# A diffusion transformer block on one core: state space work of layer 0 gathered on VectorE, with merged tables and scans

## The chip, the cores and the metric

One NeuronCore of a Trainium2 chip runs the whole program. TensorE (PE) multiplies matrices, VectorE (DVE), ScalarE (ACT) and GpSimd (POOL) do the elementwise work, and SyncE (SP) issues the transfers. The metric is the device time of one execution in microseconds (us), lower is better.

## The reference, cut to what matters

Two layers, each over 512 latent tokens and 256 context tokens of width 1024. Each layer conditions its normalised input with a shift and a scale from an adaptive projection (ada), mixes tokens in three ways side by side (windowed attention, a gated convolution of three taps, a bidirectional state space model), and then runs an MLP.

```python
mod = (c_act @ w_ada[l] + b_ada[l])[:, None, :]
a_lat = modulate(rms_norm(h, g_pre_mix), sh1, sc1)
...
conv = cb * centred_conv3(cc * cx, conv_w)
# s5_bidirectional
lam_bar = jnp.exp(lam * dt)
b_bar = ((lam_bar - 1) / lam)[..., None] * lax.complex(b_re, b_im)
h_lat_f = diag_scan(lam_bar[0], drive(u, 0), h_ctx_f[:, -1], False)
h_lat_b = diag_scan(lam_bar[1], drive(u, 1), h_ctx_b[:, 0], True)
y = real(einsum(hf, c_mat[0]) + einsum(hb, c_mat[1])) + d_skip * t
g = jax.nn.gelu(y)
return g * jax.nn.sigmoid(g @ w_glu + b_glu)
```

The state space model has 16 groups, 64 complex states each, two directions. Layer 1 gives no context output.

## The kernel before, in words

Every large product is made of three matmuls (`mm3`, L659 to L661) on a high and a low part of both operands, so each weight tile is split into such parts first (`wload`: cast on ACT, L643, and the subtraction of the low part, L644, in turn on DVE and POOL).

The tokens are cut into chunks of 8, 96 chunks in all (`NCH`; 32 of them context). The state space model is done in two halves of 8 groups. For a half, `ssm_mats` builds matrices from powers of the eigenvalues (DVE and POOL, L353 to L359; PE, L367 to L387). The last products of PE give the kernel of a chunk, which goes to DRAM (`strips`) and comes back as a Toeplitz matrix (`ssm_tr`, `ssm_tm`). `ssm_scan` multiplies the input chunks by these matrices (PE, L483), turns the result by a table of phases (`ssm_table`), runs a real scan over the chunks (L503), and turns back (L513 to L520) to the state `s`. `ssm_read` adds the chunk's own part (L539) and the state's (L545) and applies the gelu.

A tile framework puts the instructions of each engine into an order of its own by a modelled timeline, and places its waits by the tiles. So the code's order is only a hint, and the orders below are what the engines get. Each engine works through its own order without overtaking.

The program in stages, by the trace: `startup` (0 to about 81 us: norms, the first two slices of the ada projection in two halves `ada_half`, conditioning of the input by `transpose_mod`, the projection `u_proj` of the state space input, and `ssm_mats`), `phase_w` of layer 0 (to 204.4 us: convolution, both scans and readouts, further ada slices, L774), attention, the MLP of layer 0 with the preparation of layer 1's matrices and tables in its shadow (`ssm_spill`), then the same of layer 1 with `phase_w` from about 1056 to 1131 us. In `transpose_mod` a letter for each block of 128 channels says which engine does what: ACT or DVE makes the conditioned block (`full`, L729 on DVE) and its high part, DVE or POOL subtracts (L734). One half of the ada projection is eight tiles of 512 KB, each used by four matmuls (L817), whose sum is added to a bias (L820), transposed and made into the scale `A` (L829).

Of the kernel before, what the change touches and what calls it, by code (L numbers as in the profile page):

```python
# [95 lines left out]
def ssm_params(E, a):  # L96
# [196 lines left out]
def ssm_table(E, l, d, a0, na, tab):  # L293

    nc = E.nc
    V, G = nc.vector, nc.gpsimd
    c0 = (l * 2 + d) * 8 + a0
    cs = slice(c0, c0 + na)
    tb = tab if d == 0 else tab[:, :, :, ::-1]
    G.memset(tb[:, 0, :, 0:1], 1.0)  # L300
    G.memset(tb[:, 1, :, 0:1], 0.0)
# [2 lines left out]
    while m < NCH:
        n = min(m, NCH - m)
        wrb, wib = bc(wr, 2, n), bc(wi, 2, n)
        t1 = E.mp.tile([P, 8, 32], F32, name="ssm_tt", tag="ssm_y", bufs=2)[:, :na, :n]
        t2 = E.mp.tile([P, 8, 32], F32, name="ssm_tt", tag="ssm_y", bufs=2)[:, :na, :n]
        ar, ai = tb[:, 0, :, 0:n], tb[:, 1, :, 0:n]
        o_r, o_i = tb[:, 0, :, m:m + n], tb[:, 1, :, m:m + n]  # L310
        V.tensor_mul(o_r, ar, wrb)
        G.tensor_mul(t1, ai, wib)
        V.tensor_sub(o_r, o_r, t1)
        G.tensor_mul(o_i, ar, wib)
        G.tensor_mul(t2, ai, wrb)
        V.tensor_add(o_i, o_i, t2)
        m *= 2
        if m < NCH:
            nw = E.mp.tile([P, 4, 8], F32, name="ssm_w", tag="ssm_w", bufs=2)[:, :, :na]
            V.tensor_mul(nw[:, 2], wr, wr)  # L320
            V.tensor_mul(nw[:, 3], wi, wi)
            V.tensor_sub(nw[:, 0], nw[:, 2], nw[:, 3])
            V.scalar_tensor_tensor(out=nw[:, 1], in0=wr, scalar=2.0, in1=wi, op0=OP.mult, op1=OP.mult)
            wr, wi = nw[:, 0], nw[:, 1]
# [648 lines left out]
def block(E, l, cols):  # L973
    tc, nc, a = E.tc, E.nc, E.a
    with psum_phase(E, f"w{l}", s=3, a=1, m=4) as E.pp, \
# [548 lines left out]
```

## Time and profile before

| | us |
|---|---|
| median of three runs (lowest, highest) | 1680.35 (1680.06, 1680.41) |
| the profiled execution | 1681.77 |
| its span in the trace | 1679.9 |
| PE busy in the span | 1569.0 |
| DVE, ACT, POOL busy | 904.7, 538.8, 502.8 |

The span is the stretch from the first to the last instruction of the trace, and 1.87 us of the profiled execution lie outside it. Busy time is the time in which an engine runs at least one instruction. PE's instructions are pipelined, so a busy PE is not PE at its best, and its granted clock is 1.00 or 0.50 of full speed in a stretch.

### The profile page before, as it was taken

The numbers are of one execution on the slowest core, as the hardware profiler recorded it, in microseconds if no ns is written. First come the engines' busy times: TensorE is split into PE (matmuls) and PEld (weight loads), VectorE is DVE, ScalarE is ACT, GpSimd is POOL, SyncE is SP. The second block draws the span as 40 slices with busy tenths as digits, with TensorE's granted clock in tenths as the row PEclk, the third lists the DMA queues.
The fourth block names the chain that finished last, engine by engine and source line by source line (L and its number), as shares of the span: only waits on it lengthen the run. The fifth ranks groups of instructions, "written<-read, shape, count | busy, mean of one in ns | idle before, by whom it ended". The sixth has DMA issues, their size and how long they took to land. (4 is left out here: it accounts for less than half of the span.)

```text
span 1679.9 us, 22886 instructions
## 1 busy us (share of the span) xinstructions
PE 1569.0 (93%) x8872; PEld 1265.2 (75%) x8872; DVE 904.7 (54%) x1949; ACT 538.8 (32%) x1005; POOL 502.8 (30%) x509
## 2 busy tenths in 40 slices
PE   5899898899899999999999997999889899999997
PEld 2587686677878888878688885778667788888885
DVE  8837626775894483323233358473774833333335
ACT  4220225553622131111213236112554522322232
POOL 5745622003372261111112125453102321222222
PEclk9888798999999999999999998979999899999999
DMA  8455422003333141162713135742302232222223
GB/s 307 154 191 184 137 70 76 1 12 128 126 114 110 44 146 60 51 221 80 251 51 100 51 138 194 278 148 85 114 1 95 84 101 98 101 100 101 90 99 125
DMA packets 73132, 193.82 MB, mean 115 GB/s; under 512 B 15168, under 2 KB 25664, under 8 KB 72768
## 3 DMA queue, kind: packets, MB, share of 16 engines
q1 hardware_dynamic: 73024, 192.37, 33.2%
q8 instruction: 69, 1.13, 0.3%
q14 instruction: 39, 0.32, 0.1%
HBM read 172.15 MB, written 20.19 MB: 114 GB/s over the span
## 5 line engine op out<-in xcount | busy, mean ns | idle before, releaser
L644 POOL TENSOR_TENSOR w<-w 128x1024 fp32r<-128x1024 f32 x86 | 208.7, 2426 | 727.8 <-ACT w L643 332.9
L643 ACT CAST w<-w 128x1024 fp32r<-128x1024 f32 x172 | 178.9, 1049 | 469.9 <-PE ps_q L660 296.0
L660 PE MATMUL ps_q<-w,f 128*128 128x512 f32 x640 | 249.9, 392 | 3.9 <-DVE w L644 3.1
L659 PE MATMUL ps_q<-w,f 128*128 128x512 f32 x640 | 247.6, 392 | 2.7 <-DVE g L1476 2.6
L661 PE MATMUL ps_q<-w,f 128*128 128x512 f32 x640 | 247.7, 391 | 0.0
L644 DVE TENSOR_TENSOR w<-w 128x1024 fp32r<-128x1024 f32 x86 | 110.4, 1283 | 147.0 <-ACT w L643 138.0
L659 PE MATMUL ps_m<-g,w 128*128 128x256 f32 (+1 forms) x544 | 177.9, 332 | 2.5 <-DVE g L731 2.4
L660 PE MATMUL ps_m<-g,w 128*128 128x256 f32 (+1 forms) x544 | 179.4, 331 | 0.0
L661 PE MATMUL ps_m<-g,w 128*128 128x256 f32 (+1 forms) x544 | 177.9, 330 | 0.0
L660 PE MATMUL ps_m<-f,w 128*128 128x512 f32 (+1 forms) x464 | 172.0, 371 | 2.0 <-DVE f L734 1.6
L659 PE MATMUL ps_m<-f,w 128*128 128x512 f32 (+1 forms) x464 | 171.1, 372 | 1.5 <-ACT f L725 1.2
L661 PE MATMUL ps_m<-f,w 128*128 128x512 f32 (+1 forms) x464 | 170.2, 368 | 0.0
L1482 DVE TENSOR_TENSOR g<-g,ps_q 128x1024 f32<-128x1024 f32 x60 | 73.3, 1221 | 177.3 <-PE ps_q L661 177.3
L660 PEld LDWEIGHTS ps_q<-w,f 128*128 128x128 f32 x640 | 120.7, 189 | 30.4 <-DVE w L644 4.6
L659 PEld LDWEIGHTS ps_q<-w,f 128*128 128x128 f32 x640 | 120.2, 188 | 29.1 <-DVE g L1476 3.9
L661 PEld LDWEIGHTS ps_q<-w,f 128*128 128x128 f32 x640 | 120.7, 189 | 24.7
L659 PE MATMUL ps_m<-w,f 128*128 128x512 f32 (+1 forms) x336 | 125.2, 375 | 8.8 <-DVE p L929 4.1
L661 PE MATMUL ps_m<-w,f 128*128 128x512 f32 (+1 forms) x336 | 124.7, 372 | 0.0
L660 PE MATMUL ps_m<-w,f 128*128 128x512 f32 (+1 forms) x336 | 123.5, 369 | 0.0
L1405 DVE SCALAR_TENSOR_TENSOR relu<-ps_m,relu 128x512 f32<-128x512 f32 (+1 forms) x104 | 58.3, 564 | 118.8 <-ACT relu L1404 118.7
L1408 DVE TENSOR_TENSOR f<-relu,f 128x512 fp32r<-128x512 f32 (+1 forms) x104 | 85.1, 820 | 57.8 <-ACT f L1407 57.4
L659 PEld LDWEIGHTS ps_m<-g,w 128*128 128x128 f32 x544 | 103.7, 193 | 16.3 <-DVE g L731 3.0
(289 smaller groups left out, 2762.8 us busy)
## 6 DMA issues: line engine op xcount, KB each, us to landing
w<-in_w_ada SPq DMA_DIRECT2D x96, 512.0 KB
w<-in_w_mlp_in SPq DMA_DIRECT2D x64, 512.0 KB
w<-in_w_mlp_out SPq DMA_DIRECT2D x64, 512.0 KB
w<-in_w_out SPq DMA_DIRECT2D x16, 512.0 KB
w<-in_w_conv SPq DMA_DIRECT2D x12, 512.0 KB
h_d<-g SPq DMA_DIRECT2D x12, 512.0 KB
w<-in_w_q SPq DMA_DIRECT2D x8, 512.0 KB
f<-h_d SPq DMA_DIRECT2D x8, 512.0 KB
```

The costliest lines, as they stand in the source:

```text
L643: nc.scalar.copy(hi, raw)
L644: (nc.gpsimd if turn % 2 else nc.vector).tensor_sub(lo, raw, hi.bitcast(F32))
L659: nc.tensor.matmul(out, lh, rh, start=first, stop=False)
L660: nc.tensor.matmul(out, lh, rl, start=False, stop=False)
L661: nc.tensor.matmul(out, ll, rh, start=False, stop=last)
L1405: V.scalar_tensor_tensor(out=s, in0=pt, scalar=0.0, in1=s, op0=OP.max, op1=OP.mult)
L1408: V.tensor_sub(lo, s, hi.bitcast(F32))
L1482: V.tensor_add(facc[t], facc[t], pq)
```

## The change

- `ssm_params`, `ssm_mats`, `ssm_out_mat`, `ssm_scan`: the halves that POOL did go to DVE, two copies go to ACT.
- `ssm_table` builds one table for both directions (the backward one reads it reversed) in fewer and longer steps, all on DVE. In layer 0 it is called in `startup`.
- The scans of one direction, eight of 96 elements, become two of 384 with a zero in the decay at each edge. The turning back becomes two products of 760 elements, one difference and one sum.
- The second half's eight ada tiles of `startup` go to state space tiles that nothing uses yet, not to the pool of weight tiles. A transpose uses another PSUM tile.
- The matrices of the second half of layer 0 are made after the first half's readout, not in `startup`.
- `wload` subtracts on DVE alone up to the end of `phase_w`. `transpose_mod` in `startup` has its subtractions all on DVE, and half of its blocks made on ACT. The gelu has one DVE instruction less, one convolution tap goes to ACT, its last subtraction to DVE, two memsets to POOL. `E.steps` sets which ada steps stand between which parts.

```diff
-    wr, wi = E.w8[:, 0, cs], E.w8[:, 1, cs]
+    V.tensor_copy(tab[:, :, :, 1], E.w8[:, :, cs])
     m = 1
...
+    while m < NCH - 1:
+        k = min(m, 24, NCH - 1 - m)
+        t = E.mp.tile([P, 2, n, 24], F32, name="ssm_tt", tag="T3", bufs=2)[:, :, :, :k]
+        a, o = tab[:, :, :, 1:1 + k], tab[:, :, :, m + 1:m + 1 + k]
+        br, bi = (bc(tab[:, q, :, m], 2, k) for q in range(2))
+        for q in range(2):
+            V.tensor_mul(o[:, q], a[:, q], br)
+            V.tensor_mul(t[:, q], a[:, 1 - q], bi)
+        V.tensor_sub(o[:, 0], o[:, 0], t[:, 0])
+        V.tensor_add(o[:, 1], o[:, 1], t[:, 1])
+        m += k
...
-        G.tensor_add(z[:, 0], z[:, 0], t[:, 0])
-        G.tensor_sub(z[:, 1], z[:, 1], t[:, 1])
...
+        V.tensor_add(z[:, 0], z[:, 0], t[:, 0])
+        V.tensor_sub(z[:, 1], z[:, 1], t[:, 1])
+        rz = E.mp.tile([P, 4, NCH], F32, name="ssm_rz", tag="T3", bufs=2)
+        V.tensor_copy(rz, bc(E.r8[:, u.cs], 2, NCH))
...
-                V.tensor_tensor_scan(o, r8, i, 0.0, OP.mult, OP.add)
+            zq = z[:, q].rearrange("p k c -> p (k c)")[:, rv]
+            V.tensor_tensor_scan(zq, rf, zq, 0.0, OP.mult, OP.add)
...
-            G.tensor_copy(s[:, :, :, 0:CCH], s[:, :, :, NCH:NCH + CCH])
+            nc.scalar.copy(s[:, :, :, 0:CCH], s[:, :, :, NCH:NCH + CCH])
...
-        (nc.gpsimd if turn % 2 else nc.vector).tensor_sub(lo, raw, hi.bitcast(F32))
+        (nc.gpsimd if turn % 2 and E.wpool else nc.vector).tensor_sub(lo, raw, hi.bitcast(F32))
...
-        raw = wtile(E, [P, 2, 512])
+        if h == 0:
+            raw = wtile(E, [P, 2, 512])
+        elif kc in (4, 5, 6):
+            raw = E.xa([P, 2, 512])
...
-    E.smode = "oppooppo"
+    E.smode = "eoeoeoeo"
...
-    E.steps = ((2, 2, 2, 5, 6), (1, 1, 1, 3, 4))
+    E.steps = ((0, 2, 2, 5, 8), (1, 1, 1, 3, 4))
...
-    E.U1 = ssm_mats(E, E.S, 0, 1)
...
-        U1 = E.U1
         ssm_read(E, U0, t0, s0, u_t, 0, y_d, not both)
+        U1 = ssm_mats(E, S, 0, 1)
```

The lines of the changed kernel have other numbers. In the pieces of its orders, a name's number only tells one buffer from another.

DVE, in the conditioning of the second half of the ada projection. Before, L820 adds the bias, L827 copies the transposed sums, and L829 makes `A`, with the table's steps (L311 to L323) between:

```order
207 L820 TENSOR_TENSOR f4_454<-f4_454,ps_a_604 128x256
208 L313 TENSOR_TENSOR ssm_tab0_1026<-ssm_tab0_1026,ssm_tt_1206 128x8x32
209 L316 TENSOR_TENSOR ssm_tab0_1026<-ssm_tab0_1026,ssm_tt_1207 128x8x32
210 L320 TENSOR_TENSOR ssm_w_1237<-ssm_w_1224 128x8
211 L827 COPY mod00_398<-ps_a_654 128x2x2x2 x2
212 L321 TENSOR_TENSOR ssm_w_1237<-ssm_w_1224 128x8
213 L313 TENSOR_TENSOR ssm_tab1_1027<-ssm_tab1_1027,ssm_tt_1216 128x8
214 L323 SCALAR_TENSOR_TENSOR ssm_w_1237<-ssm_w_1224 128x8
215 L829 SCALAR_TENSOR_TENSOR A00_401<-mod00_398,vecs_75 128x2x4
```

Now the addition stands at row 228 (its line is L808), the copies are L815, `A` is L817, and L624 is the subtraction of a weight's low part, here of the convolution's:

```order
231 L624 TENSOR_TENSOR w_1009<-w_1004,w_1008 128x1024
232 L624 TENSOR_TENSOR w_1013<-w_1006,w_1012 128x1024
233 L305 TENSOR_TENSOR ssm_tab_854<-ssm_tab_854,ssm_tt_900 128x16x24
234 L306 TENSOR_TENSOR ssm_tab_854<-ssm_tab_854,ssm_tt_900 128x16x24
235 L815 COPY mod00_398<-ps_s_654 128x2x2x2 x2
236 L278 TENSOR_TENSOR ssm_t_846<-ssm_b_835,ssm_fz_85 128x256
237 L279 TENSOR_TENSOR ssm_t_847<-ssm_b_835,ssm_fz_85 128x256
238 L303 TENSOR_TENSOR ssm_tab_854<-ssm_tab_854 128x16x15 x2
239 L304 TENSOR_TENSOR ssm_tt_907<-ssm_tab_854 128x16x15 x2
240 L817 SCALAR_TENSOR_TENSOR A00_401<-mod00_398,vecs_75 128x2x4
```

Two weight subtractions and longer table steps have come between the addition and `A`, and the small squarings `ssm_w` are gone.

PE, at the end of the matrices of the second half. Before, L377 and L379 are their last products, and the first half's input products (L483, from `ssm_xt_869` and `ssm_xt_891`) and its first own part (L539) follow:

```order
364 L377 MATMUL ps_s_1012<-ssm_cb_941,ssm_x_969 128x32
365 L379 MATMUL ps_s_1012<-ssm_cb_941,ssm_x_969 128x32
366 L483 MATMUL ps_s_1302<-u_t_1025,ssm_xt_869 64x96 x8
367 L483 MATMUL ps_s_1303<-u_t_1025,ssm_xt_869 64x96 x8
368 L774 MATMUL ps_a_1033<-w_1699,cT_74 32x256 x2
...
376 L539 MATMUL ps_s_1409<-u_t_1025,ssm_tm_938 128x96
```

Now those products are L357 and L359, the input products L463, the ada steps L755 and the own part L520, and all of these are of the second half:

```order
512 L359 MATMUL ps_s_1299<-ssm_cb_1228,ssm_x_1256 128x32
513 L463 MATMUL ps_s_1419<-u_t_1002,ssm_xt_1243 64x96 x8
514 L463 MATMUL ps_s_1420<-u_t_1002,ssm_xt_1243 64x96 x8
515 L755 MATMUL ps_a_1607<-w_1802,cT_74 32x256 x4
516 L755 MATMUL ps_a_1607<-w_1803,cT_74 32x256
517 L463 MATMUL ps_s_1466<-u_t_1002,ssm_xt_1265 64x96 x8
518 L463 MATMUL ps_s_1467<-u_t_1002,ssm_xt_1265 64x96 x8
519 L755 MATMUL ps_a_1607<-w_1803,cT_74 32x256 x3
520 L755 MATMUL ps_a_1607<-w_1814,cT_74 32x256 x4
521 L755 MATMUL ps_a_1607<-w_1815,cT_74 32x256
522 L520 MATMUL ps_s_1734<-u_t_1002,ssm_tm_1515 128x96
```

The first half's scan no longer stands behind the second half's matrices, and the second half's Toeplitz matrix `ssm_tm_1515` is now used 9 rows behind the products that it is made of.

SP, behind the weights of `u_proj`. Before, three state space inputs and then the eight tiles of the second ada half (L815), each waiting for a weight tile to come free:

```order
20 L640 DMA w_518<-in_w_u 128x1024
21 L1197 DMA nsink_2174<-in_attn_sink 128x8
22 L270 DMA ssm_b_835<-in_ssm_b 128x512
23 L271 DMA ssm_c_837<-in_ssm_c 128x512
24 L288 DMA ssm_dd_851<-in_ssm_d 16x256
25 L815 DMA w_605<-in_w_ada 128x2x512
```

Now those eight (L803) come first, into state space tiles:

```order
20 L620 DMA w_518<-in_w_u 128x1024
21 L1184 DMA nsink_2028<-in_attn_sink 128x8
22 L803 DMA ada_w_605<-in_w_ada 128x2x512
...
29 L803 DMA ada_w_647<-in_w_ada 128x2x512
30 L265 DMA ssm_b_835<-in_ssm_b 128x512
31 L266 DMA ssm_c_837<-in_ssm_c 128x512
```

The ada tiles have moved ahead of the state space inputs.

## Rows read from the trace of the kernel before

**Rows 1.** The page: span, and the busy time of PE.

```profile
span 1679.9 us, 22886 instructions
PE 1569.0 (93%) x8872; PEld 1265.2 (75%) x8872; DVE 904.7 (54%) x1949; ACT 538.8 (32%) x1005; POOL 502.8 (30%) x509
```

**Rows 2.** Stretches by stage: length, busy time by engine, clock, DMA.

```profile
14.50:81.00 66.50, 55.46 (x347) 32.60 (x348) 61.30 (x182) 18.15 (x26) 53.85 (x100) 0.87 0.63 215
81.00:204.40 123.40, 114.16 (x898) 89.88 (x896) 73.36 (x122) 22.19 (x36) 66.69 (x58) 0.86 0.54 179
445.00:1000.00 555.00, 551.29 (x3054) 457.84 (x3053) 251.78 (x465) 137.50 (x228) 141.88 (x159) 0.99 0.30 105
1056.00:1131.00 75.00, 72.69 (x563) 54.60 (x563) 48.21 (x88) 14.18 (x21) 32.73 (x26) 0.89 0.64 221
```

**Rows 3.** Shorter stretches of the same view, with the clock lowered.

```profile
191.30:208.30 17.00, 14.12 (x86) 12.92 (x87) 4.37 (x8) 2.91 (x5) 5.82 (x5) 0.50 0.10 33
1102.60:1119.70 17.10, 14.94 (x88) 11.87 (x87) 14.97 (x25) 2.90 (x4) 11.73 (x10) 0.50 0.23 67
```

**Rows 4.** The same view: a window in layer 1's preparation, and the busiest of VectorE.

```profile
160.00:180.00 20.00, 19.84 (x190) 12.88 (x189) 18.23 (x33) 6.00 (x9) 15.96 (x14) 0.90 0.65 221
480.00:500.00 20.00, 18.27 (x89) 15.32 (x89) 18.62 (x54) 3.14 (x6) 15.64 (x36) 0.88 0.34 125
600.00:620.00 20.00, 20.00 (x121) 17.77 (x120) 19.37 (x92) 4.76 (x11) 15.58 (x44) 1.00 0.33 115
```

**Rows 5.** Timeline of PE: start, us, instruction, idle before and its releaser.

```profile
14.49 1.08 PE L817 MATMUL ps_a<-w,cT 128*32 128x256 f32 x8 [14.49 <-DMA w<-in_w_ada]
80.80 0.39 PE L661 MATMUL ps_m<-f,w 128*128 128x512 f32 x1
120.44 0.61 PE L379 MATMUL ps_s<-ssm_cb,ssm_x 128*128 128x32 f32 x2
120.98 2.83 PE L483 MATMUL ps_s<-u_t,ssm_xt 128*64 128x96 f32 x32
194.18 1.17 PE L545 MATMUL ps_s<-ssm_s,ssm_o 64*128 64x96 f32 x8 [7.04 <-POOL ssm_s L520]
202.49 2.03 PE L545 MATMUL ps_s<-ssm_s,ssm_o 64*128 64x96 f32 x16
1106.48 0.66 PE L539 MATMUL ps_s<-u_t,ssm_tm 128*128 128x64 f32 x2 [2.16 <-DVE ssm_zt L493]
```

**Rows 6.** Timeline of DVE, the same columns.

```profile
26.71 0.42 DVE L820 TENSOR_TENSOR f<-f,ps_a 128x256 f32<-128x256 f32 x1 [0.75 <-PE ps_a L817]
54.16 0.15 DVE L321 TENSOR_TENSOR ssm_w<-ssm_w 128x8 f32<-128x8 f32 x1
54.40 0.15 DVE L829 SCALAR_TENSOR_TENSOR A<-mod,vecs 128x8 f32<-128x8 f32 x1
61.09 2.35 DVE L321 TENSOR_TENSOR ssm_w<-ssm_w 128x8 f32<-128x8 f32 x1
74.38 1.10 DVE L734 TENSOR_TENSOR f<-t,f 128x512 fp32r<-128x512 f32 x1
122.58 0.56 DVE L490 TENSOR_TENSOR ssm_z<-ps_s,ssm_tab 128x384 f32<-128x384 f32 x1 [3.41 <-PE ps_s L483]
137.09 0.68 DVE L465 TENSOR_TENSOR ssm_o<-ssm_o,ssm_m 128x512 f32<-128x512 f32 x1
1116.34 1.10 DVE L503 TENSOR_TENSOR_SCAN ssm_zo<-ssm_r,ssm_z 128x96 f32<-128x96 f32 x4
```

**Rows 7.** Timeline of POOL, the same columns.

```profile
60.89 2.53 POOL L644 TENSOR_TENSOR w<-w 128x1024 fp32r<-128x1024 f32 x1
193.27 0.86 POOL L520 COPY ssm_s<-ssm_s 128x256 f32<-128x256 f32 x1
```

**Rows 8.** Timeline of ACT: the chunk kernel's copy out, the Toeplitz matrix's copy.

```profile
96.97 0.27 ACT L589 COPY ssm_k<-ps_s 128x128 f32<-128x128 f32 x1 [2.19 <-PE ps_s L387]
107.85 1.05 ACT L589 COPY ssm_tm<-ssm_tr 128x1024 f32<-128x1024 f32 x1 [0.89 <-DMA ssm_tr<-strips]
```

More of the change, by code (lines that the diff above doesn't have):

```diff
@@ L290, in ssm_load, with ssm_table @@
     return S
-def ssm_table(E, l, d, a0, na, tab):
+def ssm_table(E, c0, n, tab):
     nc = E.nc
     V, G = nc.vector, nc.gpsimd
[L297 to L301, printed above, removed]
-    wr, wi = E.w8[:, 0, cs], E.w8[:, 1, cs]
-    m = 1
[L304 to L324, printed above, removed]
+    cs = slice(c0, c0 + n)
+    G.memset(tab[:, 0, :, 0:1], 1.0)
+    G.memset(tab[:, 1, :, 0:1], 0.0)
+    V.tensor_copy(tab[:, :, :, 1], E.w8[:, :, cs])
+    m = 1
+    while m < NCH - 1:
[9 more added lines that the diff above has]
+        m += k
 def ssm_mats(E, S, l, half):
@@ L336, in ssm_mats @@
         for q in range(2):
-            G.tensor_copy(cb[sl, q, :, :, g], S.c[sl, q, :, half * 64:half * 64 + 64].rearrange(
+            nc.scalar.copy(cb[sl, q, :, :, g], S.c[sl, q, :, half * 64:half * 64 + 64].rearrange(
                 "p d (a i) -> p d a i", i=16))
@@ L413, in ssm_spill @@
     nc = E.nc
-    E.sp_t = E.tc.dram_tile([2, P, 2, 8, NCH], F32, name="sp_t")
+    E.sp_t = E.tc.dram_tile([P, 2, 16, NCH], F32, name="sp_t")
     E.sp_x = E.tc.dram_tile([2, 2, P, 1024], F32, name="sp_x")
@@ L488, in ssm_scan @@
         t = E.mp.tile([P, 2, 4, NCH], F32, name="ssm_zt", tag="T3", bufs=2)
-        tc_, ts_ = (S.tab[d][:, q, half * 4:half * 4 + 4] for q in range(2))
+        ks = slice(d * 8 + half * 4, d * 8 + half * 4 + 4)
+        rv = slice(None) if d == 0 else slice(None, None, -1)
+        tc_, ts_ = (S.tab[:, q, ks, rv] for q in range(2))
         V.tensor_mul(z[:, 0], dr, tc_)
@@ L731, in transpose_mod @@
             nc.vector.tensor_copy(hi, full)
-        elif p not in "op":
+        elif p not in "ope":
             nc.scalar.copy(hi, full)
@@ L778, in ada_slice @@
     rows = E.t2([P, 512])
-    V.memset(rows, 0.0)
+    nc.gpsimd.memset(rows, 0.0)
     bias = a["b_ada"][l, s * 2048:(s + 1) * 2048].rearrange("(o k b j) -> b o k j", o=1, k=2, b=4)
@@ L820, in ada_half @@
     V.tensor_add(rows, rows, pa[:, :256])
-    pt = E.pt('a')
+    pt = E.pt('s')
     for q in range(2):
@@ L1020, in startup @@
     rows = E.f4([P, 2, 256])
-    V.memset(rows, 0.0)
+    G.memset(rows, 0.0)
     for b in range(4):
@@ L1037, in startup @@
     drain(E.up)
-    E.S = ssm_load(E, a, 0)
+    S = E.S = ssm_load(E, a, 0)
+    S.tab = E.mp.tile([P, 2, 16, NCH], F32, name="ssm_tab")
+    ssm_table(E, 0, 16, S.tab)
     E.U0 = ssm_mats(E, E.S, 0, 0), ssm_tm(E, 0, 0)
-    E.U1 = ssm_mats(E, E.S, 0, 1)
     return cols
@@ L1111, in phase_w @@
     S = E.S if l == 0 else Env()
-    S.tab = [E.mp.tile([P, 2, 8, NCH], F32, name=f"ssm_tab{d}") for d in range(2)]
     if l == 1:
+        S.tab = E.mp.tile([P, 2, 16, NCH], F32, name="ssm_tab")
         U0, t0 = ssm_fill(E, 0), ssm_tm(E, 1, 0)
-        for d in range(2):
-            E.bdma(S.tab[d], E.sp_t[d])
+        E.bdma(S.tab, E.sp_t)
     else:
@@ L1158, in phase_w @@
     step(sn[2])
-    if l == 0:
-        for d in range(2):
-            ssm_table(E, 0, d, 0, 8, S.tab[d])
     s0 = ssm_scan(E, S, U0, u_t, l, 0, not both)
     if both:
-        U1 = E.U1
         ssm_read(E, U0, t0, s0, u_t, 0, y_d, not both)
+        U1 = ssm_mats(E, S, 0, 1)
         conv("cc", wcc)
```

74 lines of the change are left out of this document (34 added, 40 removed).

## The prediction

> **What bounds the kernel now.** I read the page first: PE is busy in 1569.0 of 1679.9 us [rows 1], so over the whole program PE is the limit, and a change on other engines pays only in a stage where PE waits or runs at the lower clock. The view by stretches says which. In the MLP of layer 0 PE is busy in 551.29 of 555 us at a clock of 0.99 [rows 2]: there is nothing to be had there but in a few windows. In startup after the first 14.5 us, PE is busy in 55.46 of 66.50 us at a clock of 0.87, and in phase W of layer 0 in 114.16 of 123.40 at 0.86 [rows 2]. The losses there, idle time and the lost share of the clock together, are 11.0 + 0.13 x 66.5 = 20 us and 9.2 + 0.14 x 123.4 = 26 us. Phase W of layer 1 loses 2.3 + 0.11 x 75 = 11 us [rows 2]. The change works in these three places.
>
> Next, who is waited for. In startup, DVE is busy in 61.30 of the 66.50 us [rows 2], so it sets the pace there. The timelines of DVE and POOL side by side show why it is so slow: a DVE instruction on 8 elements takes 2.35 us at 61.09, where the same one takes 0.15 at 54.16 [rows 6]. It ends at 63.44, and the POOL subtraction that began at 60.89 ends at 63.42 [rows 7]. DVE stands still until POOL is through. Between the first half's adding of the bias at 26.71 and the last subtraction of the conditioning at 74.38 [rows 6] there are 122 DVE instructions, and I summed what each took beyond the fastest of its own form: 15.2 us. In phase W the chain goes back and forth between DVE and POOL, and its end is seen on PE: 7.04 us idle at 194.18 for the POOL copy L520 [rows 5, 7], then the readout at half clock, in the stretch from 191.3 to 208.3 [rows 3].
>
> **Startup.** At the fastest duration of each form, those 122 instructions cost 31.1 us; they took 48.8 (26.71 to 75.48). In the order of the change, the same stretch (first L820 to last L734) has 99 instructions: 24 of conditioning 12.2 us, the table's steps 12.5, four weight subtractions 4.6 (1.14 each), six instructions of the first matrices 3.6, the rest 4.5; together 37.4 us. So POOL's work costs DVE 6.3 us more, and the standing still goes. If DVE never waits, the conditioning is done at 26.71 + 37.4 = 64.1, not 75.5. `A` of the second half comes at 26.71 + 26.0 = 52.7 against 54.40 now [rows 6]; so the earlier ada loads bring only 1.7 us by themselves, and most of the rest lies behind `A`, where 11.4 us of DVE work stand for 21.1. PE now ends u_proj at 81, some 5.5 us behind DVE's last part [rows 5, 6]. I take 4, so 68: **13 us earlier**. Bounds: nothing (if other waits of the same size take over) and 16.
>
> **Phase W of layer 0.** Here DVE's work grows. From the conditioning to the copy of the chunk kernel of the second half's matrices there are 50.3 us of DVE work at undisturbed durations, then 23.2 us for the second half's scans, against 54.8 for the whole phase now. A POOL product of 512 elements becomes one of about 0.60 net on DVE (0.68 with the overlap, L465 at 137.09 [rows 6]). Merging the scans saves little: four of 96 take 1.10 us together, a plain product of 384 takes 0.56 [rows 6], so one scan of 384 lies between 0.56 and 1.10; I take 0.85, and eight of them save 2 us, of which the four copies for the decay take back 1.1.
>
> [...] No row here shows a scan of 384.
>
> PE's order is what decides. Before, the first half's scan stands behind the second half's matrices on PE: these end at 121.0, and only then L483 starts [rows 5]. Now it follows its own matrices, and the second half's come after the first readout. How long do 50.3 us of DVE work take? DVE is busy in 73.36 of 123.40 us in this phase (0.59) and in 18.23 of 20 where it is densest [rows 2, 4]. I take 0.66, since the exchange with POOL falls away but that with PE stays: 76 us, so the second half's matrices are done at T = 64.1 + 76 = 140. Bounds 0.59 and 0.9: T = 149 and 120. From T on: 3 us of L483, 23 of scans, 10 for the last readout (194.18 to 204.5 now, at half clock [rows 3, 5]), and 5 for waits that I can't name: the phase ends at T + 42 = 182, with bounds of 191 and 162. Against 204.4 that is **22 us**, the 13 of startup within it.
>
> One wait is new. On PE the second half's L539 (now L520) stands nine rows behind the last product of its own matrices, some 3 to 4 us. The matrix must go to DRAM and back for it: now this took 10.9 us, from the copy at 96.97 to the Toeplitz copy at 107.85 [rows 8]. So PE will stand for about 7 us there, and six ada loads wait on SP behind the same transfer. I count it at nothing, because PE has about 20 us of work from there to the end, and the scan chain on DVE takes 26: the wait lies beside that chain. Were the chain shorter, up to 7 us would show.
>
> **Layer 1.** In its phase W the readout runs at half clock from 1102.6 to 1119.7 [rows 3], 8.5 us lost, with PE idle for 2.16 us behind DVE at 1106.48 [rows 5]. The change takes POOL out of that chain and mixes the readout with other products. Nothing to 10.7 us; I take **4 us**. In the preparation of layer 1 in the MLP, the work moved to DVE is hidden beneath PE (20.00 of 20 from 600 to 620, beside a DVE of 19.37); from 480 to 500 PE loses 1.73 us and 0.12 of the clock while DVE and POOL are both near full [rows 4]. **2 us** of those 4. The convolution tap and the copies on ACT cost nothing: it is busy in 22.19 of 123.40 us in phase W [rows 2]; without that cover they are about 4 us.
>
> **The sum.** 22 + 4 + 2 = 28 us from the profiled execution's 1681.77, that is 1653.8; the median stood 1.4 lower, so 1652.3.
>
> **Rivals.**
> 1. DVE becomes the limit by itself. For it: 37.4 and 73.5 us of DVE work where there were 31.1 and 54.8. If half of the 15.2 us of standing still is not POOL's, the conditioning ends at 71.7, and at a share of 0.59 T becomes 157 and the phase's end 199: 5 us there, 4 and 2 elsewhere, 1669. Against it: the two ends at 63.4 agree within 0.02 us [rows 6, 7].
> 2. The second half's matrices come so late that their chain ends the phase behind where it ends now. The mechanism is serial: matrices, L483, scans, readout, T + 42. It gives back all gains, those 6 of the other places too, when T passes 168, and the time is slower by 0.2% from T = 172. That needs a DVE share of 0.47, or PE's wait for the Toeplitz matrix and the loads behind it outside the chain. With T = 178, the time is 1690. Against it: PE has convolution and ada products for filling, and these now stand between.
> 3. It goes better: at a share of 0.9, T = 120, the phase ends at 162, and layer 1 gives 8 us with the clock up: 1680.35 - 42 - 8 - 2 = 1628. For it: the half clock of 191.3 to 208.3 and of 1102.6 to 1119.7 goes with small products and waits of PE [rows 3, 5], and both get fewer.
> 4. The gains and the longer chains cancel, within 0.2% (about what a measurement of this kernel can tell from no change): T near 166.
>
> **How the numbers follow.** My forecast, 1652 (its own range 1642 to 1662), 0.50; rival 1 0.22 (1662 to 1676); rival 2 0.13; rival 3 0.09; rival 4 0.06. Faster is the forecast, rivals 1 and 3: 0.81; same 0.06; slower 0.13. The range leaves out rival 2 and most of 3: 1637 to 1677.
>
> **What the profile after would show.** DVE instructions of 8 to 64 elements no longer above 0.5 us before 80 us; the last L734 of startup at 64, u_proj's end at 68; L463 of the first half soon after its matrices, near 90; the second half's matrices done near 140; an idle PE of up to 7 us before the second half's first own part; the last readout of phase W near 182, and every stage behind it shifted by the same amount until layer 1's phase W. A last L734 after 72 or T after 160 would make the forecast wrong; so would a longer attention or MLP, of which the change touches nothing but weights loaded ahead.

## The result and the profile after

The change makes the kernel faster: 1657.45 us (median of four runs, 1652.46 to 1662.5) against 1680.38 (four runs, 1680.06 to 1682.44), a ratio of 0.9861 with a 95% interval of 0.983 to 0.9892. The forecast was 1652 in a range of 1637 to 1677. The profiled execution took 1657.21. First its page: span and busy time, to be read beside [rows 1]. PE's busy time fell by 9.6 us and POOL's by 200.

```profile
span 1655.4 us, 22621 instructions
PE 1559.4 (94%) x8872; PEld 1258.4 (76%) x8872; DVE 900.2 (54%) x1986; ACT 552.5 (33%) x1037; POOL 302.5 (18%) x231
```

The view by stretches, columns as in [rows 2]: length, PE, weight loads, DVE, ACT, POOL, clock, DMA share, GB/s. In order: the two stretches of [rows 2] in startup and phase W of layer 0, the MLP, all from 14.5 us to the end of phase W of layer 0, and phase W of layer 1 (from the last transpose of the handover to the first product of the attention, L1231 in before and L1218 in after).

```profile
14.50:81.00 66.50, 59.02 (x379) 37.81 (x380) 56.15 (x186) 28.33 (x45) 3.17 (x6) 0.95 0.66 229
81.00:204.40 123.40, 119.54 (x1032) 96.09 (x1031) 79.86 (x146) 27.76 (x52) 11.14 (x18) 0.96 0.56 184
445.00:1000.00 555.00, 545.70 (x2941) 448.27 (x2939) 255.56 (x523) 147.28 (x245) 88.28 (x52) 0.99 0.32 113
14.50:181.00 166.50, 157.33 (x1245) 113.37 (x1245) 128.93 (x309) 50.02 (x83) 9.95 (x17) 0.95 0.64 217
1019.42:1114.01 94.59, 92.44 (x661) 72.07 (x661) 55.90 (x88) 20.09 (x32) 11.12 (x20) 0.87 0.60 204
```

The same view of before for the last two, cut at the same instructions:

```profile
14.50:204.50 190.00, 169.72 (x1245) 122.53 (x1245) 134.66 (x304) 40.34 (x61) 120.54 (x158) 0.87 0.57 191
1048.62:1137.52 88.90, 85.10 (x661) 66.54 (x660) 55.50 (x98) 18.30 (x31) 41.30 (x40) 0.90 0.62 215
```

The last two rows of after and these two hold most of the result. From 14.5 us to the end of phase W of layer 0, both kernels have the same 1245 matmuls, and after needs 23.5 us less for them. PE idles 9.2 us in place of 20.3 (11.1 less), and it is busy 12.4 us less, with a mean clock of 0.95 in place of 0.87; in the trace the half clock holds for 17 us in place of 51. Phase W of layer 1, with the same 661 matmuls, takes 5.7 us **more**. Between them the attention of layer 0 gives 3.3 us (168.6 to 165.9 and 93.0 to 92.4 for its two parts) and the MLP 2.4 (582.5 to 580.1); the attention of layer 1 and all behind it give another 1.0. The sum is -23.5 - 3.3 - 2.4 + 5.7 - 1.0 = -24.5, which is the way from 1679.9 to 1655.4.

The timeline of PE (start, us, instruction, idle before and its releaser), for [rows 5]. L463 is the old L483, L520 the own part, L526 the state's part (old L545):

```profile
91.97 1.32 PE L463 MATMUL ps_s<-u_t,ssm_xt 128*64 128x96 f32 x14
...
148.15 2.83 PE L463 MATMUL ps_s<-u_t,ssm_xt 128*64 128x96 f32 x32
...
155.88 0.46 PE L520 MATMUL ps_s<-u_t,ssm_tm 128*128 128x96 f32 x2 [1.37 <-ACT ssm_tm L569]
...
175.91 0.69 PE L520 MATMUL ps_s<-u_t,ssm_tm 128*128 128x96 f32 x4
...
179.88 1.14 PE L526 MATMUL ps_s<-ssm_s,ssm_o 64*128 64x96 f32 x16
```

The first half's scan starts at 91.97, where it started at 120.98; the second half's matrices are done at 148.2. The last readout runs at full clock, 16 products in 1.14 us where they took 2.03 before, without a wait in front, and ends at 181.0 instead of 204.5. The timeline of DVE, for [rows 6]: the second half's `A`, the last subtraction of the conditioning (L715, old L734), the scans of 384, and in front two steps of the table, for comparison below.

```profile
34.24 0.42 DVE L303 TENSOR_TENSOR ssm_tab<-ssm_tab 128x256 f32<-128x256 f32 x1
37.38 0.55 DVE L304 TENSOR_TENSOR ssm_tt<-ssm_tab 128x384 f32<-128x384 f32 x1
...
51.30 0.15 DVE L817 SCALAR_TENSOR_TENSOR A<-mod,vecs 128x8 f32<-128x8 f32 x1
...
66.74 0.68 DVE L715 TENSOR_TENSOR f<-t,f 128x512 fp32r<-128x512 f32 x1
...
98.16 0.95 DVE L485 TENSOR_TENSOR_SCAN ssm_z<-ssm_rz,ssm_z 128x384 f32<-128x384 f32 x1
...
113.29 1.80 DVE L485 TENSOR_TENSOR_SCAN ssm_z<-ssm_rz,ssm_z 128x384 f32<-128x384 f32 x2
```

Summing what each DVE instruction took beyond the fastest of its own form, between 28 and 60 us, gives about 10.9 us before and 0.9 after. By what is counted as one form, these sums and those further down move by a few us; the step from before to after stays.

### The profile page after: what moved, and what is told of

Read it like the earlier page. It is cut to its first block, busy times and chain, and to the rows that moved or that the text cites. A ratio compares the mean times of both kernels' runs of the same rounds, so it can differ in the third digit from the quotient of the medians.

```text
span 1655.4 us, 22621 instructions
## 1 busy us (share of the span) xinstructions
PE 1559.4 (94%) x8872; PEld 1258.4 (76%) x8872; DVE 900.2 (54%) x1986; ACT 552.5 (33%) x1037; POOL 302.5 (18%) x231
## 4 chain that ended last, share of the span: by engine, by line
PE 77%; DVE 13%; ACT 4%; DMA 3%; issue 2%; POOL 1%; SPq 0%; DVEq 0%; ACTq 0%; POOLq 0%
PE ps_m L639 14%; PE ps_m L641 14%; PE ps_m L640 14%; PE ps_q L640 8%; PE ps_q L639 8%; PE ps_q L641 8%; PE ps_a L755 3%; ACT p L872 2%; PE ps_s L526 2%; PE ps_t L897 2%; DVE p L864 1%; DMA w<-in_w_ada 1%; DVE p L877 1%; PE ps_t L890 1%; DMA ssm_tr<-strips 1%
## 5 line engine op out<-in xcount | busy, mean ns | idle before, releaser
L624 POOL TENSOR_TENSOR w<-w 128x1024 fp32r<-128x1024 f32 x79 | 193.1, 2444 | 785.9 <-ACT w L623 345.0
L624 DVE TENSOR_TENSOR w<-w 128x1024 fp32r<-128x1024 f32 x93 | 115.9, 1247 | 150.2 <-ACT w L623 136.7
L641 PEld LDWEIGHTS ps_q<-w,f 128*128 128x128 f32 x640 | 120.5, 188 | 24.9
L639 PE MATMUL ps_m<-w,f 128*128 128x512 f32 (+1 forms) x336 | 124.0, 371 | 8.9 <-DVE p L917 4.0
L641 PE MATMUL ps_m<-w,f 128*128 128x512 f32 (+1 forms) x336 | 123.4, 369 | 0.0
L640 PE MATMUL ps_m<-w,f 128*128 128x512 f32 (+1 forms) x336 | 121.8, 364 | 0.0
L639 PEld LDWEIGHTS ps_m<-g,w 128*128 128x128 f32 x544 | 103.1, 192 | 16.0 <-DVE g L712 3.0
L640 PEld LDWEIGHTS ps_m<-g,w 128*128 128x128 f32 x544 | 104.2, 192 | 11.5 <-issue 1.6
```

The lines of the kernel that those rows point to most:

```text
L624: (nc.gpsimd if turn % 2 and E.wpool else nc.vector).tensor_sub(lo, raw, hi.bitcast(F32))
L639: nc.tensor.matmul(out, lh, rh, start=first, stop=False)
L640: nc.tensor.matmul(out, lh, rl, start=False, stop=False)
L641: nc.tensor.matmul(out, ll, rh, start=False, stop=last)
```

## Experiments

All are timed beside the kernel before, whose median lay at 1681.3, 1680.5, 1683.2 and 1682.0 in the four groups. One kernel's runs spread by up to 6 us about their median. The landmarks come from each trace: **T** is the end of the second half's matrices, **end** that of the last readout of layer 0, **idle** the longest wait of PE between T and the end, **W1** the length of layer 1's phase W.

| kernel | us | ratio to before (95%) | T | end | end - T | idle | W1 |
|---|---|---|---|---|---|---|---|
| before | 1680.38 | 1 | 121.0 | 204.5 | - | 7.0 | 88.9 |
| after | 1657.45 | .9861 (.983, .9892) | 148.2 | 181.0 | 32.8 | 1.4 | 94.6 |
| e1_mats_early | 1679.79 | .9989 (.9972, 1.0006) | 112.7 | 198.0 | - | 7.7 | 101.7 |
| e8_before_moved | 1688.07 | 1.0041 (1.0027, 1.0054) | 160.9 | 207.6 | 46.7 | 13.2 | 92.5 |
| e10_scan_moved | 1672.75 | .9934 (.991, .9957) | 157.4 | 203.7 | 46.3 | 9.6 | 85.9 |
| e3_pool_back | 1662.93 | .9899 (.9881, .9918) | 153.8 | 186.0 | 32.2 | <0.3 | 91.9 |
| e2_wtile_loads | 1665.05 | .9908 (.9882, .9935) | 149.4 | 191.0 | 41.6 | 4.9 | 94.4 |
| e9_steps_old | 1661.86 | .9882 (.9851, .9912) | 151.5 | 194.0 | 42.5 | 6.0 | 92.4 |
| e5_dummy_two | 1683.56 | 1.0017 (1.0003, 1.0031) | 163.2 | 205.5 | 42.3 | 5.2 | 94.5 |
| e6_dummy_set | 1672.64 | .9957 (.994, .9974) | 151.9 | 194.5 | 42.6 | 5.0 | 100.2 |
| e7_read_bank | 1659.9 | .9885 (.9867, .9903) | 149.1 | 182.2 | 33.1 | 0.8 | 96.6 |
| e13_scan_bank | 1670.37 | .992 (.9902, .9938) | 150.8 | 188.2 | 37.4 | 4.2 | 104.5 |
| e14_pool_l1 | 1657.34 | .9862 (.9841, .9882) | 148.5 | 182.0 | 33.5 | 1.3 | 94.0 |
| e12_l1_old | 1654.5 | .9838 (.9818, .9858) | 146.4 | 179.6 | 33.2 | 0.7 | 91.9 |

Each landmark is of one profiled execution. The last four have after's order in layer 0 unchanged; with after itself, the same program ended phase W between 179.6 and 188.2.

### The order of the second half's matrices

**e1_mats_early** takes back the move alone:

```diff
+    E.U1 = ssm_mats(E, E.S, 0, 1)
...
-        U1 = ssm_mats(E, S, 0, 1)
+        U1 = E.U1
```

> The changed kernel, but the second half's matrices of layer 0 are made in startup again. If POOL's absence is what pays (the first theory), phase W of layer 0 still ends near 181 us, at most 3 us later, and the time is 1657 to 1661 us. If it pays that the first half's scan no longer stands behind the second half's matrices (the rival), the phase ends 8 to 12 us later and the time is 1665 to 1670 us.

No gain can be told from nothing any more; that is a larger loss than either theory of the expectation allowed. The conditioning is as early as in after (last subtraction ended at 67.2), but the scan starts at 112.6, and the tail falls back into before's pattern, a long wait of PE and a readout at half clock. PE's timeline of e1, near the end of phase W:

```profile
186.89 0.75 PE L526 MATMUL ps_s<-ssm_s,ssm_o 64*128 64x96 f32 x4 [7.70 <-DVE ssm_o L445]
...
196.01 2.03 PE L526 MATMUL ps_s<-ssm_s,ssm_o 64*128 64x96 f32 x16
```

A wait of 7.70 us for the output matrix on DVE, and the readout behind it at half clock, 2.03 for 16 products. (The clock had fallen at 174.7, behind a shorter wait of 2.35 us.) A part of the loss (7.1 us) lies in layer 1, whose order changed too, though the edit is in layer 0. That it is the order shows in the other traces: e6 has e1's order there on PE and DVE and takes 100.2 us for phase W of layer 1, where e1 takes 101.7; e2, e5 and e9 have after's order there and take 92.4 to 94.5.

**e8_before_moved** makes the move alone in the kernel before, and **e10_scan_moved** adds to that the new `ssm_scan` and `ssm_out_mat`:

```diff
-    E.U1 = ssm_mats(E, E.S, 0, 1)
...
-        U1 = E.U1
+        U1 = ssm_mats(E, S, 0, 1)
```

> The kernel before with one edit: the second half's matrices of layer 0 are made after the first half's readout. POOL keeps its share, tables, scans and loads stay as they were. If the order is what pays (the theory that the early matrices suggest), L483 of the first half starts at 100 to 106 us instead of 121, phase W ends at 186 to 194 us instead of 204.5, and the time is 1662 to 1671 us. If the order pays only together with POOL's absence, the phase ends at 200 us or later and the time is 1676 to 1682 us.

> The kernel before with two edits: the second half's matrices of layer 0 after the first half's readout, and the scans and output matrices as in the changed kernel (merged, all on DVE). Startup, tables, loads and weight subtractions stay as before. With the first edit alone the second half took 47 us from the end of its matrices to the end of phase W, with 13 us of idle PE behind POOL; in the changed kernel 33. If the scan chain's way through POOL is what made the move a loss, this stretch gets 33 to 39 us, the phase ends at 192 to 199 us and the time is 1668 to 1676 us. If it was the late startup, the stretch stays above 42 us and the time is 1680 us or more.

The move alone loses 0.4%, more than either expectation said. In its trace the phase ends 3 us later than in before, and phase W of layer 1, whose order changed too, takes 3.6 us more. PE's timelines of e8 and then of e10:

```profile
197.17 1.29 PE L545 MATMUL ps_s<-ssm_s,ssm_o 64*128 64x96 f32 x8 [13.16 <-POOL ssm_s L520]
```

```profile
192.52 0.74 PE L546 MATMUL ps_s<-ssm_s,ssm_o 64*128 64x96 f32 x4 [9.62 <-DVE ssm_o L465]
```

In e8 the second half comes late (T = 160.9) and PE waits 13 us for POOL's copy. With the new scan that releaser is gone, and DVE's output matrix takes its place. What e10 gains over before, 0.7%, is not gained here (its phase ends at 203.7) but behind it: 3.5 us in the MLP, 3.0 in layer 1's phase W and 2.5 in its attention (its edits change the MLP's preparation and the scan of layer 1 as well). So its expectation came out half and half: the stretch from T stays at 46 us, as the theory of the late startup had it, but the time is far below that theory's 1680.

### VectorE beside GpSimd

**e3_pool_back** gives POOL its halves back in the table, the matrices and the sums of the scan, and its share of the subtractions, with the old way of the conditioning:

```diff
-            V.tensor_mul(t[:, q], a[:, 1 - q], bi)
+            G.tensor_mul(t[:, q], a[:, 1 - q], bi)
...
-        (nc.gpsimd if turn % 2 and E.wpool else nc.vector).tensor_sub(lo, raw, hi.bitcast(F32))
+        (nc.gpsimd if turn % 2 else nc.vector).tensor_sub(lo, raw, hi.bitcast(F32))
...
-    E.smode = "eoeoeoeo"
+    E.smode = "oppooppo"
```

> The changed kernel, but POOL does its old share again: half of the table's products, of the matrices' and the output matrices' products, the two sums ahead of the scans, every second weight subtraction and the subtractions of the old conditioning mode. The order of the stages, the merged tables and scans and the early loads stay. If DVE's standing still beside POOL is the cost (the first theory), most of the gain goes: phase W of layer 0 ends at 193 to 203 us, small DVE instructions of startup take over 0.5 us again, and the time is 1668 to 1680 us. If order and loads are what pays, the time stays within 1657 to 1663 us.

DVE's excess between 28 and 60 us is back (10.3 us), `A` comes at 56.9 in place of 51.3, and the phase ends 5 us later. But the time is only 5.5 us above after, with intervals that overlap: as the second reading of the expectation had it, the standing still is real and costs little here by itself.

**e5_dummy_two** and **e6_dummy_set** put idle work on POOL behind the first `A` of startup; nothing else uses it:

```diff
+        if h == 0:
+            G.tensor_copy(dm[:, 0, :4], M.mod[0][:, 0, 0:4])
+            for j in range(24):
+                G.tensor_sub(dm, dm, dm)
```

In e6 the two last lines are `for j in range(60)` and `G.memset(dm, float(j))`.

> The changed kernel with 24 useless subtractions of 384 elements on POOL behind the first half's conditioning in startup, some 24 us of POOL work that reads SBUF and that nobody waits for. If POOL makes DVE stand still, DVE instructions between 28 and 55 us get longer by 8 to 20 us in sum, A of the second half comes at 58 to 68 us instead of 51.3, and the time is 1661 to 1670 us. If the two do not disturb each other, A stays at 51 to 53 us and the time at 1655 to 1660 us.

> The same as the useless subtractions, but with 60 memsets of 384 elements on POOL, which read nothing, about as long in sum. If any POOL work makes DVE stand still, A of the second half comes as late as with the subtractions. If only POOL work that reads SBUF does, A stays at 51 to 53 us and the time at 1655 to 1660 us.

POOL's timeline of e5, then DVE's beside it, then POOL's of e6 and DVE's beside that:

```profile
27.76 25.57 POOL L1022 TENSOR_TENSOR ssm_dm<-ssm_dm 128x384 f32<-128x384 f32 x24
```

```profile
40.53 1.05 DVE L303 TENSOR_TENSOR ssm_tab<-ssm_tab 128x256 f32<-128x256 f32 x1
...
46.81 1.18 DVE L304 TENSOR_TENSOR ssm_tt<-ssm_tab 128x384 f32<-128x384 f32 x1
```

```profile
29.25 28.56 POOL L1022 MEMSET ssm_dm<- 128x384 f32 x60
```

```profile
35.59 0.42 DVE L303 TENSOR_TENSOR ssm_tab<-ssm_tab 128x256 f32<-128x256 f32 x1
```

Beside subtractions, a DVE step that takes 0.42 takes 1.05, and one of 0.55 takes 1.18: about as long as POOL's own instructions, which take 25.57 / 24 = 1.07 us each. The excess is 13.5 us, `A` comes at 63.2. Beside memsets of the same size the step stays at 0.42, the excess is 1.5 and `A` comes at 53.2. So it is not POOL's being busy (25.57 us in e5, 28.56 in e6), but what it does. Which property of the subtractions makes the difference, the two runs don't show.

Both lose more than startup does, and both times lie above what their expectations gave for them. In e6 the last subtraction ends 2.7 us later than in after, and the phase 13.5; 15.2 us of the time went. It falls into the other pattern of the tail, and layer 1 into e1's order.

### The loads and the ada steps

**e2_wtile_loads** loads the second ada half through the weight tiles again, **e9_steps_old** takes the old `E.steps`:

```diff
-        if h == 0:
+        if True:
```

```diff
-    E.steps = ((0, 2, 2, 5, 8), (1, 1, 1, 3, 4))
+    E.steps = ((2, 2, 2, 5, 6), (1, 1, 1, 3, 4))
```

> The changed kernel, but the second half's eight ada tiles of startup go through the pool of weight tiles again. By the prediction's sum the early loads are worth some 2 us: L817 of the second half moves from 51.3 to at most 55 us, and the time is 1657 to 1661 us. If they are what pays in startup, A comes at 56 us or later and the time is 1665 us or more.

> The changed kernel with the old distribution of the ada steps in layer 0. If the chain of matrices, scans and readouts sets the end of phase W, the ada steps only fill, and the end stays at 181 to 185 us and the time at 1655 to 1661 us. If the fill between the second half's matrices and its readout is what keeps PE at full clock, the phase ends at 187 us or later, with over 10 us at half clock at its end, and the time is 1663 us or more.

The loads by themselves are worth 0.8 us at `A` (52.1 against 51.3) and 2.1 at the end of the conditioning (69.5). But both runs end the phase 10 and 13 us later than after, with T later by only 1.2 and 3.3. So `A` is where e2 was expected, but the time isn't; and e9's phase and half clock came as the second reading had it, with a time 1 us below its 1663. PE's timeline of e9, and its stretch from T to the end, which stands beside the same stretch of after in the fence behind it:

```profile
182.49 0.74 PE L526 MATMUL ps_s<-ssm_s,ssm_o 64*128 64x96 f32 x4 [5.97 <-DVE ssm_o L445]
```

```profile
151.50:194.00 42.50, 35.70 (x291) 28.77 (x290) 29.34 (x49) 7.77 (x12) 7.17 (x4) 0.78 0.35 114
```

```profile
148.20:181.00 32.80, 31.43 (x312) 23.14 (x311) 29.21 (x47) 7.25 (x10) 5.72 (x4) 0.96 0.62 206
```

DVE has the same work in both, 29.3 and 29.2 us. In after PE has 21 more matmuls to do there and is busy but for 1.37 us; in e9 it has done them before, waits 5.97 us from 176.5 on, and has the clock at 0.5 for 17 us from 180.5. These two rows show the two patterns. The number of products left for the tail does not decide between them: by the same view, e2 has 305 there and falls into the second pattern, e3 has 307 and stays in the first.

What does go with the patterns is when DVE is through with the last output matrix, for which the last state products wait. DVE's timelines of after and then of e9:

```profile
174.25 0.68 DVE L448 TENSOR_TENSOR ssm_o<-ssm_o,ssm_m 128x512 f32<-128x512 f32 x1
```

```profile
183.31 0.69 DVE L448 TENSOR_TENSOR ssm_o<-ssm_o,ssm_m 128x512 f32<-128x512 f32 x1
```

It ends 26.7 us behind T in after and 32.5 in e9. In front of it, DVE's order has 7 instructions of other work (convolution, weights, ada) in after and 15 in e9. From there to the end of the phase it is 6.1 us in after, with the last readouts at full clock, and 10.0 in e9, at half clock. So of the 9.6 us between the two, 5.8 are DVE's chain and 3.9 the rest behind it. The other traces divide in the same way: 24.9 to 27.6 and then 5.6 to 7.4 us in after, e3, e7, e12 and e14, 31.7 to 36.7 and then 10.0 in e2, e5, e6, e8, e9 and e10. No run changes DVE's order alone, so this is read from the traces and not tested.

In the time less of it arrives: of the 13 us, the profiled execution of e9 kept 8.2, since its attentions and layer 1's phase W were 5 us shorter, and its median lies 4.4 us above after's, with overlapping intervals.

### Layer 1

The first readout of layer 1 in after, PE's timeline. Its 64 state products use 64 rows of the array each, one half of the 128 that the own part's products use (64*128 here, 128*128 for L520).

```profile
1077.24 1.10 PE L526 MATMUL ps_s<-ssm_s,ssm_o 64*128 64x64 f32 x8
...
1080.36 1.97 PE L526 MATMUL ps_s<-ssm_s,ssm_o 64*128 64x64 f32 x8
...
1095.64 1.97 PE L526 MATMUL ps_s<-ssm_s,ssm_o 64*128 64x64 f32 x8
...
1102.26 1.11 PE L526 MATMUL ps_s<-ssm_s,ssm_o 64*128 64x64 f32 x16
```

Here 8 products take 1.10 us, where in the second readout 16 take 1.11. In the second one the two PSUM tiles, one for each half of the rows, alternate; in the first one all of one tile come first, then all of the other. In before, 28 of the 64 ran in such pairs (the last row here with all 16 of its products, the one above it with 12 of 14), at half clock:

```profile
1112.10 1.97 PE L545 MATMUL ps_s<-ssm_s,ssm_o 64*128 64x64 f32 x14
...
1115.04 1.97 PE L545 MATMUL ps_s<-ssm_s,ssm_o 64*128 64x64 f32 x16
```

And in after the clock is at 0.5 from 1079.5 to 1100. **e7_read_bank** lets the two tiles alternate, by another PSUM bank for them in layer 1; **e13_scan_bank** does it by another bank for the second scan:

```diff
-    pys = [E.pt(E.ps) for _ in range(2)]
+    pys = [E.pt('m' if lat_only else E.ps) for _ in range(2)]
```

```diff
-        pd = [E.pt(E.ps) for _ in range(2)]
+        pd = [E.pt('m' if lat_only and half else E.ps) for _ in range(2)]
```

> The changed kernel, but the readout of layer 1 takes both of its PSUM tiles from the four of the convolution's tag, so that the matmuls of the two row halves alternate in PE's order. In the changed kernel the first readout of layer 1 runs one half after the other, and 8 of its L526 take 1.97 us at half clock, as long as 16 do where the halves alternate. If that is what layer 1 lost, the first readout gets 8 to 11 us shorter and the time is 1646 to 1651 us. If the lower clock alone sets it (the rival), the readout takes as long as before and the time is 1655 to 1660 us.

> The changed kernel, but in layer 1 the second half's scan takes its PSUM tiles from the convolution's four, so that both tiles of the first readout are free at once and the matmuls of the two row halves alternate; both readouts keep their tiles, and layer 0 is untouched. If the halves one after the other are what layer 1 lost, the first readout takes 5 to 10 us instead of 20, phase W of layer 1 gets 5 to 9 us shorter and the time is 1648 to 1653 us. If transfers or DVE hold the phase as they did with the other edit of the tiles, PE waits instead and the time is 1655 to 1661 us.

In e7, the first readout alternates (16 in 1.11 us) and PE is busy 7.5 us less in phase W of layer 1, but nothing is won. PE's timeline:

```profile
1049.77 4.11 PE L463 MATMUL ps_s<-u_t,ssm_xt 128*64 128x96 f32 x48 [4.86 <-DMA u_t<-u_d]
...
1087.47 1.12 PE L520 MATMUL ps_m<-u_t,ssm_tm 128*128 128x64 f32 x4 [5.34 <-ACT ssm_tm L569]
```

It waits for the state space input and for the second half's Toeplitz matrix, 11.6 us idle in all. In e13, PE idles 23.8 us, for ada weights, for the same input and for the scan; it is slower than after, though 7 us of that lie in layer 0, which the edit leaves as it was. Neither came out as expected: e7's time lies where its rival had it, but with the readout shortened, and e13's lies above both its ranges. And neither edit is the alternation alone: beside it, 157 (e7) and 237 (e13) of the some 660 PE instructions of the phase moved in the order, where 37 moved in e1 and 49 in e14.

**e14_pool_l1** and **e12_l1_old** differ from after in layer 1's phase W alone: e14 gives POOL its share of the weight subtractions there (`E.wpool = l == 1`), e12 uses before's `ssm_scan` in addition.

```diff
-        E.wpool = False
+        E.wpool = l == 1
```

```diff
-    s0 = ssm_scan(E, S, U0, u_t, l, 0, not both)
+    s0 = (ssm_scan if both else ssm_scan_old)(E, S, U0, u_t, l, 0, not both)
...
-        s1 = ssm_scan(E, S, U1, u_t, l, 1, not both)
+        s1 = ssm_scan_old(E, S, U1, u_t, l, 1, not both)
```

> The kernel after with one change: in phase W of layer 1, POOL again takes every second subtraction of a weight's low part (wload, L624), as in the kernel before. On every engine the order is that of the kernel after up to layer 1's phase W, so only that phase (last handover transpose to the first L1231: 88.9 us before, 94.6 after) and what follows can move. In its PE order the first readout is still two blocks of 32 state products that use one half of the array's rows each, but between the two blocks stand 11 or so full products of 512 columns and three rows of ada steps, where the kernel after has two full products and seven ada steps. Theory A (the loss of layer 1 is TensorE's lowered clock, which fell at the first block and did not rise before the second was through: 20.5 us of half clock in one stretch): the clock comes back between the two blocks, half clock in the phase falls from 24 to about 10 us and the phase takes 86 to 89 us; in all 1650 to 1652. Theory B (the loss is the products' own order, 64 state products with one half of the rows each): the same 64 are there, the phase stays at 93 to 95 and the time at 1656 to 1658. Theory C (POOL beside DVE costs the chain of layer 1): the phase grows beyond 95, with DVE instructions longer in it; the time is over 1659.

> The kernel after with the scan of the kernel before in layer 1 alone (its POOL halves, eight scans of 96, turning back in two pairs) and POOL's share of the weight subtractions in layer 1's phase W. On every engine the order is that of the kernel after up to layer 1's phase W. In its PE order the two blocks of 32 state products of the first readout stand with one ada step between them, and nothing else. Theory A (the loss is the lowered clock over those two blocks): the clock stays low through both as in the kernel after, the phase takes 94 to 98 us and the time is 1657 to 1661, although the scan is the one of before. Theory B (the loss is the new scan's, which works on DVE alone): the phase is back at 88.9 or less and the time at 1652. DVE's and POOL's rows in the phase should show the scan's products on POOL and DVE instructions above the fastest of their form again, by 5 us or so together.

Phase W of layer 1 by stretches, of e14, e12, e1, e7 and e10 (each its own fence, columns as above):

```profile
1021.59:1115.62 94.03, 92.13 (x661) 73.08 (x662) 52.48 (x85) 20.18 (x32) 18.95 (x23) 0.85 0.61 210
```

```profile
1019.40:1111.27 91.87, 89.74 (x661) 70.38 (x661) 50.48 (x93) 20.20 (x32) 38.95 (x39) 0.89 0.61 211
```

```profile
1035.94:1137.68 101.74, 97.02 (x660) 76.99 (x661) 55.66 (x88) 19.97 (x32) 12.54 (x20) 0.82 0.56 196
```

```profile
1021.72:1118.31 96.59, 84.97 (x661) 68.39 (x662) 54.03 (x88) 20.04 (x32) 11.11 (x20) 0.86 0.65 210
```

```profile
1043.79:1129.69 85.90, 84.47 (x661) 66.45 (x661) 54.00 (x90) 18.63 (x30) 22.18 (x24) 0.94 0.65 226
```

What did the clock take? In before PE was busy for 14.9 us at half clock in this phase [rows 3]. I count half of that, 7.5 us, as what full clock would have saved; this is an estimate, and rather a high one, since 8 of the products above took 1.97 us at half clock and 1.10 at full, a ratio of 1.79. Without it, before's work is 85.1 - 7.5 = 77.6 us. The same from the other traces gives 80.5 us in after, 78.6 in e14, 79.5 in e12, 79.8 in e1, 79.4 in e10, and 73.8 in e7, which alternates. All but before and e7 have the first readout's halves one behind the other throughout, and all of them need more than before, by 1 to 3 us. The order of the halves can be priced by the rows above: 28 products at 1.10/8 - 1.11/16 = 0.068 us are 1.9 us, an estimate that lies within these but explains none of their differences. Counted as half of the busy time at half clock, the clock took 7.5 us in before, 12.0 in after, 13.6 in e14, 10.2 in e12, 17.3 in e1 and only 5.1 in e10, although the readout there is in the same two blocks. In e14 the clock did come back between the blocks, at 1084.7, as the theory of the clock wanted, but it fell again in the second block and once more in the second readout: 27 us of half clock in the phase, none saved, with phase and time where theory B had put them. e12 lies between its two theories. So by this count the loss in layer 1 is part order and part clock, and which order keeps the clock up could not be told beforehand. e12 is the fastest kernel measured, but its interval overlaps after's, and it isn't told apart from it.

## Why the prediction came out right

The number was right (1652 in 1637 to 1677 against 1657.45), and the largest term of the sum was met within 2 us. But that term was met by luck, since two errors in it cancel, and the term for layer 1 had the wrong sign.

- **Startup, 13 us forecast: about 8 to 9.** `A` was put at 52.7 and came at 51.3. The last subtraction was put at 64.1 and ended at 67.4, before at 75.5. PE reached the first transposes of the matrices at 70.74 instead of 79.72. The work was sized well: from the first L808 at 25.33 to 67.42, DVE was busy for 37.8 us, where the forecast had 37.4. What failed is "if DVE never waits": it waited 4.2 us there, for ACT's blocks (2.40 us in front of the subtraction at 59.58). That POOL's subtractions make DVE stand still is shown by e5 beside e6 (a DVE step of 0.42 us took 1.05 beside subtractions and 0.42 beside memsets).
- **T, forecast 140: 148.2.** 148.2 - 67.4 = 80.8 us, where the forecast had 76; with the 3.3 us from startup that makes the difference. DVE was busy for 51.5 us of the 80.8, a share of 0.64 where 0.66 was taken.
- **T + 42, forecast: T + 32.8.** This is the term whose error made up for the one before. The forecast had 3 of L483, 23 of scans, 10 for a readout at half clock and 5 for unnamed waits (which add up to 41, not 42). In after the readout takes 5.1 (175.91 to 181.0), and of the waits only the 1.37 us below come. The table shows two patterns: 32 to 33.5 us in after, e3, e7, e12 and e14, and 41.6 to 46.7 wherever PE waited about 5 us or more in one piece and read out at half clock (37.4 once in between, in e13). The forecast had sized the second and met it in e2, e5, e6 and e9 within 1 us. Which of the two a kernel gets, its order decides, and nothing in the forecast told that.
- **The end of the phase, forecast 182: 181.0**, 23.5 us earlier, by two errors of 8 and 9 us that cancel.
- **The scan of 384, taken as 0.85: 0.95**, in a pair 0.90 each, against 1.10 for four of 96 [rows 6]. 0.95 is 1.7 times the plain product's 0.56. For each further element the scan grows faster too: from 96 to 384 elements by (0.90 - 1.10/4)/288, some 2.2 ns each, and a plain product from 256 to 384 by (0.55 - 0.42)/128, some 1.0 ns; both are estimates from these rows. The merging saves 0.15 each, about what the copies of the decay cost (0.35 for two scans, L479 at 112.36).
- **The new wait for the Toeplitz matrix, up to 7 us, counted at nothing: 1.37** at 155.88. PE had 6.3 us of input products and ada steps ahead of it (148.15 to 154.5), where the forecast had 3 to 4, and the matrix came 7.7 us behind T, not 11.
- **The MLP, 2 us: 2.4.**
- **Attention of layer 0, counted at nothing: 3.3 us gained.** The change touches no code there; no experiment was made for it.
- **Layer 1's phase W, 4 us of gain forecast: 5.7 us of loss.** This is the step that failed: "Nothing to 10.7 us; I take 4 us", from taking POOL out of the chain and mixing the readout with other products. The bounds excluded a loss. The half clock grew from 17 to 24 us in place of vanishing (4.5 us more by the count above), the other work of PE grew by 2.9 us, of which some 1.9 are an estimate for the halves that stopped alternating, and 1.7 us of idle time were saved.

Of the rivals, the first (DVE limits itself) is refuted for the excess: it went from 10.9 to 0.9 us, and of DVE's instructions of 8 to 64 elements between 20 and 80 us none takes over 0.5 us any more, where ten did. The second was the right worry: in e8, with T = 160.9, the serial chain ends later than in before (T + 46.7).

What did the change's parts do? All without the move can't be told from nothing (e1, 0.9972 to 1.0006), the move without the rest costs 0.4% (e8), both together give 1.4%. The pieces don't add: the move lets the first half's scan start 29 us earlier (91.97 against 120.98) and puts the matrices of the second half behind it, so that their chain now ends the phase. As far as these runs go, it ends early enough only with the shorter startup and with a tail in which DVE reaches the last output matrix early; e10 has the new scan without them, and its phase ends where before's does. Which of the other parts pays how much isn't shown: taking back POOL's share, the loads or the ada steps (e3, e2, e9) costs 4 to 8 us each, with intervals that overlap after's. Open is why the clock falls in one order of layer 1 and holds in another. Open is also what a faster DVE chain in the tail would do to the clock by itself, since the late chain, the wait and the half clock came together in every run: in e1, e2, e5 and e6 the clock fell behind a wait of 2.4 to 3.9 us, before the longest one began, and in before, e8, e9 and e10 within the longest one.

## What to carry to other kernels

Where two halves of a serial chain share engines, ask for each half what stands between its own links; a move that is right for the chain can lose until the link beside it is shortened, so test both alone and together. In the stretch where the last link of such a chain ends the stage, look at the order of the engine that makes it: eight more small instructions in front of the last output matrix went with 6 us of delay, a wait of TensorE of 6 us and 17 us of half clock (e9 beside after). And a scheduler's order elsewhere can move by an edit that doesn't touch it: compare the stages that should not change first. Here phase W of layer 1, which e1 and e6 don't touch, took 100 to 102 us in the order that they brought and 92 to 95 in after's.

## What the runs showed of the hardware that was not expected

- In layer 1 of after, state products on one half of the array's rows ran two at a time where the halves alternate (the starts of such a pair lie 7 ns apart, those of the pairs some 105): 16 of 64x64 took 1.11 us, against 8 in 1.10 where they don't. The order alone doubled the price of these products.
- Beside two-input subtractions on POOL of 1.07 us each, a DVE step of 0.42 us took 1.05 and one of 0.55 took 1.18 (e5); beside memsets they took 0.42 and 0.55 as without them (e6).
- The same program of layer 0 ended between 179.6 and 188.2 us in five traces, and the time of one kernel spread by up to 6 us about its median, so differences under some 5 us between two such kernels need many runs.
